# Long convolutions of a Hyena branch: signals kept channel-major, blocks folded about their middle, two matmuls per residue forward and 128-column inverses

## The chip, the cores and the metric

One Trainium2 core runs the whole kernel; the other seven are idle. The metric is the device time of one execution in microseconds (us). Engines: PE is the TensorE matmul array, DVE is VectorE, ACT is ScalarE, POOL is GpSimd, and SP issues nearly all DMAs, in order, from one queue.

## The reference, cut to what matters

One encoder layer runs on two groups of rows that share weights: a prompt of 512 positions and a sample of 1024 positions, 1024 features each. In each group a projection gives, among others, 1536 channels for the Hyena branch. Per channel and order, a signal is convolved with a long filter as long as the sequence in both directions, by a zero-padded FFT:

```python
def _fftconv(u, hf, skip):
    L = u.shape[1]
    uf = jnp.fft.rfft(u.astype(jnp.float32), n=2 * L, axis=1)
    y = jnp.fft.irfft(uf * hf[None], n=2 * L, axis=1)[:, :L]
    return y + u * skip

u = _dwconv(hy_in, hy_short_w, hy_short_b)          # 3 taps
v, x1, x2 = jnp.split(u, HYENA_ORDER + 1, axis=-1)  # 512 channels each
zb = x1 * _fftconv(v, filt[:, 0], hy_skip[0])
zb = x2 * _fftconv(zb, filt[:, 1], hy_skip[1])
y_b = jnp.einsum('blc,cd->bld', zb, hy_out_w)
```

Around it stand a 31-tap convolution branch, the gated sum of both branches, an output projection with a layer norm, and a squared-ReLU MLP with a layer norm. All of it is float32.

## The kernel before, in words

**The transform.** A signal of length L is cut into L/128 blocks of 128 positions (`nt`: 4 blocks for the prompt, 8 for the sample). The transform of length 2L is done in two steps. Butterflies over the blocks on DVE (`even8`, `odd8`, called by `fwd_bfly`) leave one complex block for each of 4 (prompt) or 8 (sample) residues of the frequency. Then each residue's block is multiplied on PE with 128x128 tables of cosines and sines (`fwd_mm`: four float32 matmuls per residue, two of them accumulating into the real part and two into the imaginary part). `conv_core` takes two residues at a time, loads the filter's spectrum `ks` from DRAM into a tile `sg`, and multiplies on DVE (two products and two sums per pair). `inv_mm` returns to blocks, `inv_bfly` undoes the butterflies and ends with the multiplication by x1 or x2.

**Layouts.** Before the change the signals are turned to positions on partitions: `to_tokens` transposes the output of the 3-tap convolution `conv3` (channels on partitions, tile `cv`) with PE and evicts it with ACT. The forward matmuls then have a table as the stationary operand and 128 channels as columns. The first convolution's inverse has again a table as the stationary operand (four matmuls of 128 columns per residue). The second one's inverse has the spectrum as the stationary operand and two tables side by side as columns (two matmuls of 256 columns), which gives channels on partitions. The tables are symmetric about a shift of the block (`fft_sym`), so that one table serves both directions.

**Work and order.** One group has four channel chunks of 128, so there are 4 x 2 convolutions for the prompt and as many for the sample. These convolutions, the filters' spectra (`filters`), the 31-tap convolution (`conv31`) and its norm are side work: Python generators in two lanes. Main work is the projections and the prompt's MLP, `mlp(gp)`. A `Meter` counts an estimated time for each DVE and PE instruction as it is written (DVE: 0.065 us plus a cycle per column, divided by `SHARE` = 0.88; PE by columns). After each main step, `pump` writes steps of side work as long as DVE's estimate is behind PE's:

```python
        while v.us < t.us:
            live = [i for i in range(2) if self.side[i]]
            if not live:
                break
```

So the estimates decide how far the side work is spread over the main work. Main work goes on through both input projections, the prompt's branches and output projection, and into `mlp(gp)`, which stops as soon as no side work is left; if side work is left when `mlp(gp)` has ended, it is written in a loop with no main work beside it:

```python
                while self.side[0] or self.side[1]:
                    self.step(min((i for i in range(2) if self.side[i]), key=lambda i: self.spent[i]))
```

Then the pools of the side work close and the sample's second half follows: `branches(gs)` first, which loads what the side work has left in DRAM (`d_ca` of the 31-tap branch, `d_zb` of the Hyena branch), splits each tile into a rounded part and a rest (ACT, then DVE, tiles `pg`), and starts its matmuls with them; then the output projection and the MLP by seven products. When `mlp(gp)` has steps left there, these loads and splits are written beside them. The framework gives each engine its own instruction list and waits by semaphores; engines run their lists in order. Pools are rings: `fx` has 3 PSUM banks, `sg` 6 buffers, `fp` 11, `so` 5.

Of the kernel before, what the change touches and what calls it, by code (L numbers as in the profile page):

```python
# [60 lines left out]
def fft_tables():  # L61


    n = np.arange(128)[:, None].astype(np.float64)
    k = np.arange(128)[None, :].astype(np.float64)
    h = k[:, :64]
    c0, s0 = np.cos(2 * np.pi * n * h / 128), np.sin(2 * np.pi * n * h / 128)
    s0[:, 0] = (-1.0) ** np.arange(128)
    c8, s8 = np.cos(2 * np.pi * n * (h + 0.5) / 128), np.sin(2 * np.pi * n * (h + 0.5) / 128)
    first = [np.hstack([c0, c8]), np.hstack([c0, -c8]), np.hstack([s0, s8]), np.hstack([s0, -s8])]  # L70
    w = np.ones((64, 1))
    w[0] = 0.5
    back = [np.vstack([w * c0.T, c8.T]), np.vstack([w * c0.T, -c8.T]), np.vstack([w * s0.T, s8.T]), np.vstack([w * s0.T, -s8.T])]
    plain, sym = list(first), first + back
    for k1 in TILES_S[1:]:
        d = k1 / 16.0
        for dst, e in ((plain, 0.0), (sym, d)):
            a = 2 * np.pi * np.fmod((n + e) * (k + d), 128.0) / 128
            c, s = np.cos(a), np.sin(a)
            dst += [-s, c, s] if k1 == 6 else [s, c, -s]  # L80
    return tuple(np.ascontiguousarray(np.stack(t, axis=1).astype(np.float32)) for t in (plain, sym))
# [80 lines left out]
class Enc:  # L162
# [135 lines left out]
    def fwd_mm(self, ti, ev, q, ps):  # L298
# [12 lines left out]
        else:  # L311
            o = self.fft0 + 3 * (ti - 1)
# [18 lines left out]

    def conv_core(self, g, o, c, ev, q):

        nc, v = self.nc, self.V
        ys = []
        kny = self.sm([1, CW], tag="kny")
        nc.sync.dma_start(kny, g.kny[o, c])
        for pr in range(len(g.tiles) // 2):
# [3 lines left out]
            for j in range(2):  # L342
                self.fwd_mm(2 * pr + j, ev, q, ps[:, j])
# [8 lines left out]
            ys.append(t1)  # L352
        return ys

    def inv_mm(self, g, ys, chan_major):

        nc, t, f = self.nc, self.T, self.fft
        outs = []
        for pr, y in enumerate(ys):
# [3 lines left out]
            for j in range(2):  # L363
                ti = 2 * pr + j
                yr, yi = y[:, j, 0], y[:, j, 1]
                if ti == 0:
                    m = 4
                    mr, mi = (m, m + 1), (m + 2, m + 3)
                else:
                    m = self.fft0 + 3 * (ti - 1)  # L370
                    mr, mi = (m + 1, m + 2), (m, m + 1)
                if chan_major:
                    p = ps[:, j].rearrange("p a b -> p (a b)")
# [1456 lines left out]
```

## Time and profile before

| what | value |
|---|---|
| median of 3 runs (lowest to highest) | 2349.55 us (2346.08 to 2349.87) |
| the profiled execution, its own time | 2351.76 us |
| its span, first to last instruction | 2350.0 us |
| PE busy | 2267.9 us (97%) |
| DVE busy | 1890.1 us (80%) |
| ACT busy | 920.5 us (39%) |
| mean granted TensorE clock | 0.993 |

The span is 1.8 us shorter than the profiled execution's own time; the median of the runs is 2.2 us below that own time. A float32 matmul stands in the profile as two records (768 in the program are 1536 in the trace), a transpose or a matmul of rounded (`fp32r`) tiles as one. Matmul records overlap: "mean ns of one" holds the way through the array too, so the cost of one in a row of many is read from how long the row of many takes.

### The profile page before, as it was taken

To read this page: it belongs to the slowest core of one execution; us is meant where nothing else is said; L and a number is where in the kernel's file an instruction comes from. 1 tells how busy PE (TensorE), PEld (TensorE's weight loads), DVE (VectorE), ACT (ScalarE), POOL (GpSimd) and SP (SyncE) were. 2 spreads that over 40 slices of the span, in tenths; PEclk is the share of its full clock that TensorE was granted. 3 is DMA by queue.
4 is the path that set the end of the run, shared out by engine and by line. 5 is a ranking of instruction groups with operands and counts; after the bars stand their busy time and mean duration, and the time that the engine had idled before them with its cause. 6 is when DMAs were issued, how large, how long until landed. Compare 5 with 4: busy or idle time off the path is not lost.

```text
span 2350.0 us, 33224 instructions
## 1 busy us (share of the span) xinstructions
PE 2267.9 (97%) x11684; PEld 1882.4 (80%) x11684; DVE 1890.1 (80%) x3662; ACT 920.5 (39%) x1521; POOL 54.3 (2%) x149
## 2 busy tenths in 40 slices
PE   6999999999999999989999999999999999999998
PEld 3878777778878888978888888789887777788886
DVE  5989797786989998895898875965987777577888
ACT  3464522422232223356543344222574444444430
POOL 2210100000000000000000000000000000000000
PEclk9999999999999999999999999999999999999999
DMA  6555434564356646634443344653675666876631
GB/s 246 179 169 175 138 113 163 195 224 159 133 188 203 200 174 215 218 116 144 144 135 99 94 157 154 210 156 109 210 247 188 215 205 214 283 241 215 205 124 71
DMA packets 201068, 412.80 MB, mean 176 GB/s; under 512 B 23321, under 2 KB 33739, under 8 KB 200389
## 3 DMA queue, kind: packets, MB, share of 16 engines
q1 hardware_dynamic: 200069, 409.67, 53.0%
q8 instruction: 92, 1.51, 0.3%
q0 software_dynamic: 832, 1.02, 0.2%
q14 instruction: 75, 0.61, 0.1%
HBM read 316.16 MB, written 94.43 MB: 175 GB/s over the span
## 4 chain that ended last, share of the span: by engine, by line
PE 79%; DVE 9%; DMA 8%; ACT 2%; issue 2%; SPq 1%; DVEq 0%; ACTq 0%
PE mm L145 57%; PE fx L145 19%; PE tr L145 3%; DVE sg L145 2%; DVE pg L145 2%; DVE wt L145 1%; DMA fp<-in_dec_s_dram 1%; DMA sg<-d_xs 1%; DMA fp<-in_w_ada_dram 1%; DVE st L145 1%; DVE fp L145 1%; DMA sg<-in_ffn_w_dram 1%; DMA sg<-ks 1%; DMA raw<-in_w_out_dram 1%; DVE xt L145 1%
## 5 line engine op out<-in xcount | busy, mean ns | idle before, releaser
L145 PE MATMUL mm<-pg,wt 128*128 128x512 f32 (+1 forms) x4776 | 1139.7, 391 | 5.0 <-DVE xt L145 3.6
L145 PEld LDWEIGHTS mm<-pg,wt 128*128 128x128 f32 x4776 | 878.7, 189 | 194.4 <-issue 11.9
L145 PE MATMUL mm<-wt,pg 128*128 128x512 f32 (+1 forms) x2556 | 480.8, 344 | 9.5 <-DVE wt L145 5.0
L145 PEld LDWEIGHTS mm<-wt,pg 128*128 128x128 f32 x2556 | 404.8, 190 | 68.6 <-DVE wt L145 6.8
L202 ACT ACTIVATE wt<-raw 128x512 fp32r<-128x512 f32 x430 | 268.7, 630 | 476.1 <-PE mm L145 375.7
L145 DVE TENSOR_TENSOR wt<-raw,wt 128x512 fp32r<-128x512 f32 x430 | 290.2, 684 | 80.0 <-ACT wt L202 78.1
L145 DVE SCALAR_TENSOR_TENSOR cv<-cv,pp 128x512 f32<-128x512 f32 (+1 forms) x288 | 288.7, 1009 | 7.3 <-ACT cv L853 2.3
L145 PEld LDWEIGHTS fx<-fp,fft 128*128 128x128 f32 x1536 | 177.5, 192 | 20.2 <-issue 15.1
L145 PE MATMUL fx<-fp,fft 128*128 128x128 f32 x1536 | 184.1, 277 | 1.7 <-DVE sm L145 1.1
L145 DVE TENSOR_TENSOR fp<-fp 128x256 f32<-128x256 f32 (+2 forms) x328 | 145.0, 481 | 15.6 <-ACT fp L380 10.2
L145 DVE TENSOR_TENSOR sg<-fx,sg 128x512 f32<-128x512 f32 (+1 forms) x162 | 98.6, 629 | 43.9 <-PE fx L145 27.7
L145 DVE TENSOR_TENSOR pg<-so,pg 128x512 fp32r<-128x512 f32 (+1 forms) x162 | 99.6, 623 | 38.3 <-ACT pg L202 26.9
L145 PE MATMUL fx<-pg,pg 128*128 128x512 f32 x492 | 120.7, 394 | 7.2 <-ACT pg L202 4.3
L145 PEld LDWEIGHTS fx<-pg,pg 128*128 128x128 f32 x492 | 93.5, 190 | 27.5 <-ACT pg L202 4.7
L202 ACT ACTIVATE pg<-so 128x512 fp32r<-128x512 f32 (+1 forms) x127 | 72.1, 575 | 73.9 <-DVE so L145 52.0
L145 PE MATMUL fx<-wt,pg 128*128 128x512 f32 x387 | 95.5, 389 | 0.0
L1260 ACT ACTIVATE so<-so,pp 128x512 f32<-128x512 f32 x62 | 44.4, 719 | 128.8 <-DVE so L145 128.7
L145 DVE TENSOR_TENSOR sg<-sg 128x256 f32<-128x256 f32 (+2 forms) x187 | 82.3, 460 | 6.4 <-ACT sg L890 5.0
L145 PEld LDWEIGHTS fx<-wt,pg 128*128 128x128 f32 x387 | 72.7, 188 | 15.1
L145 PE MATMUL mm<-pg,pg 128*128 128x512 f32 x300 | 73.9, 396 | 5.5 <-DVE xt L145 5.5
L380 ACT ACTIVATE fp<-fx 128x512 f32<-128x512 f32 x48 | 28.7, 598 | 120.6 <-PE fx L145 110.4
L145 DVE TENSOR_TENSOR pg<-pg,pg 128x1024 fp32r<-128x1024 f32 (+1 forms) x45 | 55.0, 1221 | 24.4 <-ACT pg L202 19.6
(175 smaller groups left out, 2221.4 us busy)
## 6 DMA issues: line engine op xcount, KB each, us to landing
raw<-in_mlp_w_dram SPq DMA_DIRECT2D x232, 256.0 KB
raw<-in_w_in_dram SPq DMA_DIRECT2D x144, 256.0 KB
xr<-in_mlp_w_dram SPq DMA_DIRECT2D x104, 256.0 KB
fp<-in_w_ada_dram SPq DMA_DIRECT2D x48, 512.0 KB
pg<-d_p SPq DMA_DIRECT2D x44, 512.0 KB
raw<-in_w_out_dram SPq DMA_DIRECT2D x64, 256.0 KB
d_p<-so SPq DMA_DIRECT2D x64, 256.0 KB
d_g<-so SPq DMA_DIRECT2D x48, 256.0 KB
```

Source lines behind the costliest of these rows:

```text
L145: return f(*args, **kw)
L202: self.nc.scalar.activation(hi, src, AF.Copy)
L380: nc.scalar.activation(outs[-1][:, 4 * (pr % 2):4 * (pr % 2) + 4].rearrange("p (j w) c -> p j w c", j=2), ps, AF.Copy)
L1260: nc.scalar.activation(out, src, AF.Relu, bias=self.pp[:, C_B1 + f:C_B1 + f + 1], scale=1.0)
```

## The change

Signals stay with channels on partitions. `fold` adds and subtracts, within each block, the first 64 positions and the last 64 read backwards (two DVE instructions over all blocks), so each block holds its even and its odd part about its middle. The butterflies run on that. Then PE transposes the butterflies' output, 16 blocks for the sample, 8 for the prompt, and ACT evicts each PSUM bank in two halves of 64 partitions, the lower half with its two blocks swapped. With the real part's cosine and the imaginary part's sine stacked in one table, a residue needs two forward matmuls of 128 columns (four for residue 0). The inverse always has the spectrum as the stationary operand and one table of 128 columns, two matmuls per residue, written into PSUM as two runs of 64 columns that lie apart for all residues but some. `inv_bfly` is as before; `unfold` adds and subtracts the halves again (two DVE instructions) and multiplies by x1 or x2, which stays in the tile of `conv3`. `to_tokens` is gone. The generator `hyena` hands back at more places and without numbers (they weren't used). The second table becomes `fft_sig`: 34 blocks of 128 columns where `fft_sym` had 29.

```diff
+    c, s, no = np.hstack([c0, c8]), np.hstack([s0, s8]), np.zeros((64, 128))
+    fwd = [np.vstack([c, no]), np.vstack([np.hstack([c0, -c8]), no]), np.vstack([no, np.hstack([s0, -s8])]), np.vstack([no, s])]
+    inv = [np.block([[w * c0.T, w * c0.T], [c8.T, -c8.T]]), np.block([[w * s0.T, w * s0.T], [s8.T, -s8.T]])]
...
+        a = 2 * np.pi * m * (k + d) / 128
+        c, s = np.cos(a), sign * np.sin(a)
+        fwd += [np.vstack([c, -s]), np.vstack([c, s])]
+        inv += [np.hstack([c.T, -s.T]), np.hstack([s.T, c.T])]
...
+    def fold(self, g, src):
...
+        a, b = src[:, :, 0:64], src[:, :, 127:63:-1]
+        v.tensor_tensor(x[:, 0:g.nt, 0:64], a, b, op=ALU.add)
+        v.tensor_tensor(x[:, 0:g.nt, 64:128], a, b, op=ALU.subtract)
+        return x
...
+        for pr in range(npr):
+            if pr % 2 == 0:
+                turned.append(self.fp())
+            src = q if pr >= 2 else ev
+            ps = self.fx_ps([128, 2, 2, 128])
+            for j in range(2):
+                for n, slot in enumerate(self.SLOTS[TILES_S[2 * pr + j]]):
+                    self.T.transpose(ps[:, j, n], src[:, slot], self.ident)
+            dst = turned[-1][:, 4 * (pr % 2):4 * (pr % 2) + 4].rearrange("p (j n) c -> p j n c", j=2)
+            nc.scalar.activation(dst[0:64], ps[0:64], AF.Copy)
+            nc.scalar.activation(dst[64:128], ps[64:128, :, ::-1], AF.Copy)
+        yield
...
-                self.fwd_mm(2 * pr + j, ev, q, ps[:, j])
+                x = turned[pr // 2][:, 4 * (pr % 2) + 2 * j:4 * (pr % 2) + 2 * j + 2]
+                for n in range(2):
+                    if pr == j == 0:
+                        self.T.matmul(ps[:, j, n], f[:, 2 * n], x[:, 0], start=True, stop=False)
+                        self.T.matmul(ps[:, j, n], f[:, 2 * n + 1], x[:, 1], start=False, stop=True)
+                    else:
+                        self.T.matmul(ps[:, j, n], f[:, 2 + 2 * (2 * pr + j) + n], x[:, n], start=True, stop=True)
...
-                if chan_major:
-                    p = ps[:, j].rearrange("p a b -> p (a b)")
-                    t.matmul(p, yr, f[:, mr[0]:mr[0] + 2].rearrange("p a b -> p (a b)"), start=True, stop=False)
-                    t.matmul(p, yi, f[:, mi[0]:mi[0] + 2].rearrange("p a b -> p (a b)"), start=False, stop=True)
-                else:
-                    for w in range(2):
-                        t.matmul(ps[:, j, w], f[:, mr[w]], yr, start=True, stop=False)
-                        t.matmul(ps[:, j, w], f[:, mi[w]], yi, start=False, stop=True)
+                p = ps[:, j].rearrange("p w (h n) -> p (w h) n", h=2)
+                for n, to in enumerate((slice(0, 3, 2), slice(1, 4, 2)) if ti == 0 else (slice(0, 4, 3), slice(1, 3))):
+                    self.T.matmul(p[:, to], y[:, j, n], f[:, 18 + 2 * ti + n], start=True, stop=True)
...
+    def unfold(self, g, e, mul):
...
+        a, b = e[:, 0:g.nt, 0:64], e[:, 0:g.nt, 64:128]
+        v.tensor_tensor(y[:, 0:g.nt, 0:64], a, b, op=ALU.add)
+        v.tensor_tensor(y[:, 0:g.nt, 127:63:-1], a, b, op=ALU.subtract)
+        v.tensor_tensor(y[:, 0:g.nt], y[:, 0:g.nt], mul, op=ALU.mult)
+        return y
...
-        x = self.to_tokens(g, self.conv3(g, c))
...
-        x1 = self.to_tokens(g, self.conv3(g, 4 + c))
...
+        z = blocks(self.conv3(g, c))
+        yield
+        for o in range(2):
+            x = self.fold(g, z[:, 0:g.nt])
+            yield
+            ev, q = self.fwd_bfly(g, x)
+            yield
+            ys = yield from self.conv_core(g, o, c, ev, q)
+            outs = self.inv_mm(g, ys)
+            m = blocks(self.conv3(g, 4 * (o + 1) + c))
+            yield
+            z = self.inv_bfly(g, outs, m)
+            yield
```

The instruction counts of the two programs differ so: PE has 768 -> 608 float32 matmuls fx<-fp,fft (the filters' 384 among them are untouched), 192 matmuls fx<-sg,fft of 128 columns and 96 fx<-fft,sg of 256 columns -> 192 fx<-fft,sg of 128 columns (112 of them as two runs of 64), 96 transposes fx<-ident,cv -> 192 fx<-ident,fp. DVE has 64 more instructions, 32 of 256 and 32 of 512 elements. ACT has 24 evictions fewer of 512 elements on 128 partitions and 96 more on 64 partitions.

What the estimates make of it, on PE's list. Here is the end of the side work in the program before: the last sample convolution (fx<-fp,fft is its forward, fx<-fft,sg its inverse) in the middle of `mlp(gp)`, whose matmuls are mm<-pg,wt (up) and mm<-wt,pg (down).

```order
L145 MATMUL mm<-pg,wt 128x512 x24
L145 MATMUL fx<-fp,fft 128x128 x32
L145 MATMUL fx<-fft,sg 128x256 x4
L145 MATMUL mm<-pg,wt 128x512 x4
L145 MATMUL fx<-fft,sg 128x256 x8
L145 MATMUL mm<-pg,wt 128x512 x4
L145 MATMUL fx<-fft,sg 128x256 x4
L145 MATMUL mm<-pg,wt 128x512 x64
L145 MATMUL mm<-wt,pg 128x512 x96
L145 MATMUL mm<-pg,wt 128x512 x96
L145 MATMUL mm<-wt,pg 128x512 x96
```

And here is the place in the changed program where the side work ends: the last matmuls of `mlp(gp)` (mm<-wt,pg and mm<-pg), then transposes and forward matmuls of a convolution; the sixteen inverse matmuls are cut. This piece from the first fx<-ident,fp on stands three times in a row on PE, and what follows the third is the first matmul of `branches(gs)`.

```order
L158 MATMUL mm<-wt,pg 128x512 x9
L158 MATMUL mm<-pg 128x512 x3
L158 MATMUL fx<-ident,fp 128x128 x16
L158 MATMUL fx<-fp,fft 128x128 x18
L158 MATMUL fx<-fft,sg 128x2x64 x3
L158 MATMUL fx<-fft,sg 128x128
L158 MATMUL fx<-fft,sg 128x2x64
```

Before, 520 matmuls of `mlp(gp)` come behind the last convolution (the last four rows above and 168 more). Now none do: three of the eight sample convolutions (the second of channel chunk 2 and both of chunk 3) come behind the last of them.

On DVE, the end of the last sample convolution before: the butterflies (fp<-fp), the multiplication by x2 (fp<-fp,cv), among splits for the MLP's weights (wt) and activations (pg) and additions of `mlp(gp)`'s results (pg<-pg,mm), with the first splits for `branches(gs)` (numbered pg) between them.

```order
L145 SCALAR_TENSOR_TENSOR fp<-fp 128x4x128
L145 TENSOR_TENSOR wt<-raw,wt 128x512
L145 SCALAR_TENSOR_TENSOR fp<-fp 128x2x128
L145 TENSOR_TENSOR wt<-raw,wt 128x512 x2
L145 TENSOR_TENSOR fp<-fp,cv 128x1024
L145 TENSOR_TENSOR pg<-so,pg 128x512
...
L145 TENSOR_TENSOR pg<-pg,mm 128x512
L145 TENSOR_TENSOR pg_13200<-so,pg_13200 128x512
L145 TENSOR_TENSOR pg<-pg,mm 128x512
L145 TENSOR_TENSOR pg_13205<-so,pg_13205 128x512
```

And the same place now: the end of the last one but one (its unfold, 128x8x64, and the multiplication), the fold of the last (128x8x64 again), and further down that one's end, directly followed by the sixteen splits for `branches(gs)`, which no other work stands between.

```order
L158 SCALAR_TENSOR_TENSOR fp<-fp 128x4x128
L158 SCALAR_TENSOR_TENSOR fp<-fp 128x2x128
L158 TENSOR_TENSOR fp<-fp 128x8x64 x2
L158 TENSOR_TENSOR fp<-fp,cv 128x1024
L158 TENSOR_TENSOR fp<-fp 128x8x64 x2
L158 TENSOR_TENSOR fp<-fp 128x512 x2
...
L158 TENSOR_TENSOR fp<-fp,cv 128x1024
L158 TENSOR_TENSOR pg_14083<-so,pg_14083 128x512
L158 TENSOR_TENSOR pg_14088<-so,pg_14088 128x512
L158 TENSOR_TENSOR pg_14093<-so,pg_14093 128x512
```

On DVE's list, between the last addition of `mlp(gp)` and that last multiplication, stand besides the three convolutions: 3 instructions of `conv3` and 4 of the prompt's last layer norm (1024 elements each), 6 splits of weights (512), 2 BN_STATS, 1 BN_AGGR and about 25 one-column instructions.

## Rows read from the trace of the kernel before

**Rows 1.** The page, part 1 (busy us, share of the span, instructions of each engine) and part 2 (the span in 40 equal slices, busy share in tenths).

```profile
PE 2267.9 (97%) x11684; PEld 1882.4 (80%) x11684; DVE 1890.1 (80%) x3662; ACT 920.5 (39%) x1521; POOL 54.3 (2%) x149
...
PE   6999999999999999989999999999999999999998
...
DVE  5989797786989998895898875965987777577888
```

**Rows 2.** Busy time of each engine in three stretches of the span (start:end and length in us, then busy us and instructions of each engine, granted clock, DMA share, GB/s): the side work's stretch, the rest of `mlp(gp)` behind it, and the sample's second half.

```profile
430.00:1381.00 951.00, 924.41 (x5359) 789.64 (x5358) 816.04 (x1703) 335.49 (x569) 6.95 (x72) 0.99 0.49 161
1381.00:1502.60 121.60, 117.97 (x519) 96.99 (x518) 86.51 (x148) 52.58 (x90) 0.00 (x0) 1.00 0.57 184
1502.60:2350.00 847.40, 817.92 (x3941) 682.69 (x3939) 637.10 (x1124) 349.58 (x562) 0.00 (x0) 0.99 0.58 192
```

**Rows 3.** Groups of instructions by line, engine, operation and shape (count | busy us, mean ns of one | idle before, and what ended it): PE's groups of the convolutions, ACT's evictions behind them.

```profile
L145 PE MATMUL fx<-fp,fft 128*128 128x128 f32 x1536 | 184.1, 277 | 1.7 <-DVE sm L145 1.1 <-DVE fp L145 0.2
...
L145 PE MATMUL fx<-sg,fft 128*128 128x128 f32 x384 | 47.7, 276 | 2.5 <-DVE sg L145 2.5
...
L145 PE MATMUL fx<-fft,sg 128*128 128x256 f32 x192 | 46.8, 387 | 1.9 <-DVE sg L145 1.4 <-DVE sm L145 0.3
...
L145 PE MATMUL fx<-ident,cv 128*128 128x128 f32 x208 | 31.1, 275 | 0.1
...
L380 ACT ACTIVATE fp<-fx 128x512 f32<-128x512 f32 x48 | 28.7, 598 | 120.6 <-PE fx L145 110.4 <-issue 10.3
```

**Rows 4.** PE's instructions in order of time in the last two sample convolutions (start us, us of the row of xcount instructions).

```profile
1304.12 1.04 PE L145 MATMUL fx<-ident,cv 128*128 128x128 f32 x8
1304.91 11.14 PE L145 MATMUL mm<-pg,wt 128*128 128x512 f32 x48
...
1326.07 3.75 PE L145 MATMUL fx<-sg,fft 128*128 128x128 f32 x32
...
1363.85 7.30 PE L145 MATMUL fx<-fp,fft 128*128 128x128 f32 x64
...
1374.34 3.65 PE L145 MATMUL fx<-fft,sg 128*128 128x256 f32 x16
```

**Rows 5.** DVE's instructions in order of time in the last sample convolution, from its products to its last multiplication (start us, us, in brackets idle time before it and what ended it).

```profile
1370.17 1.29 DVE L145 TENSOR_TENSOR sg<-fx,sg 128x512 f32<-128x512 f32 x2 [1.29 <-DMA sg<-ks]
1371.49 0.76 DVE L145 TENSOR_TENSOR sg<-sg 128x256 f32<-128x256 f32 x2
...
1375.17 1.29 DVE L145 TENSOR_TENSOR sg<-fx,sg 128x512 f32<-128x512 f32 x2 [0.93 <-DMA sg<-ks]
1376.92 0.43 DVE L145 TENSOR_TENSOR sg<-fp 128x256 f32<-128x256 f32 x1 [0.46 <-ACT fp L380]
...
1378.94 0.48 DVE L145 TENSOR_TENSOR fp<-sg 128x128 f32<-128x128 f32 x2
...
1381.30 2.77 DVE L145 TENSOR_TENSOR fp<-fp 128x512 f32<-128x512 f32 x8 [0.53 <-ACT fp L380]
...
1388.30 1.22 DVE L145 TENSOR_TENSOR fp<-fp,cv 128x1024 f32<-128x1024 f32 x1
1389.44 0.68 DVE L145 TENSOR_TENSOR pg<-so,pg 128x512 fp32r<-128x512 f32 x1
```

**Rows 6.** Groups of DVE by shape, as in rows 3; the COPY reads its 1023 elements backwards.

```profile
L145 DVE TENSOR_TENSOR fp<-fp 128x512 f32<-128x512 f32 x100 | 63.9, 682 | 3.3 <-ACT fp L380 1.9 <-ACT fp L817 1.4
...
L145 DVE COPY fp<-fp 128x1023 f32<-128x1023 f32 x1 | 0.7, 694 | 0.0
```

**Rows 7.** The chain of work that ended last, in order of time, around the end of the side work (start us, us, what).

```profile
1366.38 3.70 DMA sg<-ks
...
1380.63 93.41 PE mm L145 x412
```

**Rows 8.** What PE waited for before instructions of `fx` (in total us, times, longest).

```profile
PE fx L145 <- DVE sg L145: 6.7, 9, 1.4
...
PE fx L145 <- DVE fp L145: 3.2, 4, 1.5
```

**Rows 9.** Two stretches of 5 us; in the first PE had only transposes for the prompt's first layer norm to do, with waits between them (columns as in rows 2: the first busy time is PE's, the number behind POOL's is the granted clock).

```profile
1045.00:1050.00 5.00, 2.62 (x16) 1.82 (x14) 5.00 (x21) 3.42 (x5) 0.00 (x0) 0.96 0.00 0
1050.00:1055.00 5.00, 4.98 (x28) 4.49 (x29) 4.12 (x15) 3.76 (x8) 0.00 (x0) 0.70 0.00 0
```

**Rows 10.** PE and DVE in order of time at the end of `mlp(gp)` and the start of `branches(gs)`; sm<-sm are one-column instructions of the prompt's last layer norm.

```profile
1496.64 0.21 DVE L145 TENSOR_SCALAR sm<-sm 128x1 f32<-128x1 f32 x1
1496.77 0.68 DVE L145 BATCH_NORM_STATS2 st<-pg 128x6 f32<-128x512 f32 x1
...
1500.12 1.28 DVE L145 SCALAR_TENSOR_TENSOR pg<-pg,sm 128x1024 f32<-128x1024 f32 x1
...
1501.31 0.15 DVE L145 TENSOR_SCALAR sm<-sm 128x1 int32<-128x1 int32 x1
...
1502.62 27.59 PE L145 MATMUL mm<-pg,wt 128*128 128x512 f32 x121
```

**Rows 11.** SP's queue in order of time, from the last result of the side work to the last load of it for `branches(gs)`.

```profile
1389.55 0.33 SPq L841 DMA_DIRECT2D d_zb<-fp  x1
...
1396.95 1.85 SPq L903 DMA_DIRECT2D so<-d_ca  x4
...
1410.36 3.03 SPq L903 DMA_DIRECT2D so<-d_zb  x4
```

More of the change, by code (lines that the diff above doesn't have):

```diff
@@ L330, in spectrum_to @@
             nc.sync.dma_start(g.ks[o, c, pr], kt)
+    def fold(self, g, src):
+        v = self.V
+        x = self.fp()
+        a, b = src[:, :, 0:64], src[:, :, 127:63:-1]
+        v.tensor_tensor(x[:, 0:g.nt, 0:64], a, b, op=ALU.add)
+        v.tensor_tensor(x[:, 0:g.nt, 64:128], a, b, op=ALU.subtract)
+        return x
     def conv_core(self, g, o, c, ev, q):
-        nc, v = self.nc, self.V
-        ys = []
+        nc, v, f = self.nc, self.V, self.fft
+        npr = len(g.tiles) // 2
         kny = self.sm([1, CW], tag="kny")
         nc.sync.dma_start(kny, g.kny[o, c])
-        for pr in range(len(g.tiles) // 2):
+        turned = []
+        for pr in range(npr):
[10 more added lines that the diff above has]
+        yield
+        ys = []
+        for pr in range(npr):
             kt = self.sg([128, 2, 2, CW])
@@ L352, in conv_core, with inv_mm @@
             ys.append(t1)
+        yield
         return ys
-    def inv_mm(self, g, ys, chan_major):
-        nc, t, f = self.nc, self.T, self.fft
+    def inv_mm(self, g, ys):
+        nc, f = self.nc, self.fft
         outs = []
@@ L806, in conv3 @@
         return t
[L808 to L818 removed]
     def hyena(self, g, c):
         nc = self.nc
[L823 to L842 removed]
+        blocks = lambda t: t.rearrange("p (a b) -> p a b", b=128)
+        z = blocks(self.conv3(g, c))
[10 more added lines that the diff above has]
+            z = self.inv_bfly(g, outs, m)
+            yield
+        nc.sync.dma_start(g.d_zb[c], z[:, 0:g.nt].rearrange("p a b -> p (a b)"))
     def conv31(self, g, c):
@@ L1769 @@
 _INS = ["x_prompt", "x_sample", "pp", "w_ada", "b_ada", "w_in", "w_y", "w_out", "mlp_w1", "mlp_w2", "ffn_w1", "ffn_w2", "ffn_w3",
-        "skip", "ln1_g", "ln1_b", "mlp_b2", "ln2_g", "ln2_b", "fft", "fft_sym", "z_p", "z_s", "dec_p", "dec_s"]
+        "skip", "ln1_g", "ln1_b", "mlp_b2", "ln2_g", "ln2_b", "fft", "fft_sig", "z_p", "z_s", "dec_p", "dec_s"]
 _OUTS = [((512, D), "float32"), ((1024, D), "float32")]
@@ L1808, in layout @@
         o[k] = i[k][0]
-    o["fft"], o["fft_sym"] = fft_tables()
+    o["fft"], o["fft_sig"] = fft_tables()
     for n, L in (("p", 512), ("s", 1024)):
```

76 lines of the change are left out of this document (20 added, 56 removed).

## Prediction

> **What bounds the kernel now.** First the busy shares: PE 97%, DVE 80%, and PE's slices stay at 9 or 8 nearly throughout [rows 1], so at first sight every microsecond taken from PE is a microsecond of time. Then the stretches: where the convolutions lie, from 430 to 1381 us, PE is busy for 924 of 951 us, but DVE for 816 (86%); it is the second limit there, 135 us behind [rows 2]. Then the chain: behind the last convolution it is an unbroken row of main matmuls, 412 in 93.4 us, 0.227 us each [rows 7]. So the side work ends early enough to leave PE something to do, and DVE's slowness costs nothing. That cover has to be watched, since the order of both programs is known.
>
> **What the change takes from PE.** Costs of one are read from rows of many: a record of a 128-column float32 matmul takes 7.30/64 = 0.114 us forward and 3.75/32 = 0.117 us inverse, one of 256 columns 3.65/16 = 0.228, a transpose (1304.91 - 1304.12)/8 = 0.099, say 0.11 [rows 4]. The groups' means are a little higher (184.1/1536 = 0.120, 31.1/208 = 0.150), since the ends of short rows count in them [rows 3]. Forward: 160 matmuls, 320 records, 36.5 us less. Inverse: 384 x 0.117 + 192 x 0.228 = 88.7 us before, 384 x 0.117 = 44.9 now, 43.8 less. Transposes: 96 more, 10.6 us. Together 69.7 us less on PE (73 by the groups' means, 66 if the short rows are worse than I read them). A matmul written as two runs of 64 columns is not in the trace; it lies between the contiguous one of 0.117 and the one with twice the columns, 0.228. I take 0.117: the runs are long, and the columns are the same.
>
> On this very term the Trainium skill speaks against the change: its page "PSUM — Partial Sum Buffer", Specifications (TRN2), says that an access pattern which isn't contiguous slows matmuls significantly. It gives no size and no run here shows one; it is a rival below.
>
> **What it adds to DVE.** A row of DVE instructions advances by 0.60 us per 512 elements (1.29 for two less 0.69), 0.34 per 256, 0.20 per 128, 1.14 per 1024 [rows 5], although each is listed with 0.68 [rows 6]. The 64 additions cost 32 x 0.34 + 32 x 0.60 = 30 us. Reading backwards isn't dearer: the reversed copy took 694 ns for 1023 elements, about the 682 of a sum of 512 [rows 6]. If it were, a step of 1.2 us would be the upper bound, 0.6 us more on each.
>
> **What else moves, at no cost.** ACT gets 96 evictions of 64 partitions for 24 of 128; at 0.60 us each [rows 3] that is 43 us on an engine that works 335 of 951 us there [rows 2]. The larger table (34 blocks for 29) loads under main matmuls. PE's new waits, transposes for the butterflies, take the place of the forward matmuls' waits for the same results, 3.2 us in all [rows 8]; I add 2 us.
>
> **What the order does with it.** The meter sees PE's side work cheaper and DVE's dearer, so it spreads the side work over more main work, and main work runs out: three sample convolutions stand behind the last matmul of `mlp(gp)`, alone. Before, 520 main matmuls came behind the last one. So most of PE's gain is handed to a stretch in which PE waits for DVE. Its length decides.
>
> One convolution costs DVE, by the code, 17 instructions of 512 elements, 31 of 256, 20 of 128, the last one of 1024 and a one-row product: 17 x 0.60 + 31 x 0.335 + 20 x 0.20 + 1.14 + 0.20 = 26.0 us. Of the first of the three, fold and butterflies (7.7 us) are done beforehand: 18.3. The other DVE work listed there: 7 x 1.19 + 6 x 0.60 + 2 x 0.60 + 0.12 and 25 one-column instructions at 0.13 [rows 10] = 16.6. Together 18.3 + 52.0 + 16.6 = 87 us.
>
> DVE will not be busy all the time. In the last convolution before, it waited 1.29 and 0.93 us for the spectrum `ks`, whose load takes 3.7 us [rows 7] and can start only when a ring buffer is free, and 0.46 and 0.53 for evictions: 3.2 us [rows 5]. New is the wait from the last butterfly to the first product, now that nothing stands between: 8 transposes and six matmuls, 8 x 0.11 + 12 x 0.114 = 2.25 us, with the hops some 2.5. So 5.7 us at full clock. PE works only some 9.6 us per convolution (16 x 0.11 + 36 x 0.114 + 32 x 0.117). Where it had just 2.6 of 5 us to do, its granted clock was 0.70 in the next 5 us, that is, part of the time at 1.2 instead of 2.4 GHz [rows 9]; I expect the lower level in much of the tail. The 2.25 us above and two inverses of a pair on the way (0.94 each) would take twice as long, 4.1 us more: 9.8. I take 8 for each of the last two and 3 for the first, where the norm's instructions fill in: 19. The tail is then 106 us (99 to 112).
>
> Behind it `branches(gs)` starts with nothing prepared: sixteen tiles are to be split, the first five loaded beforehand, and the last channel's result has to go to DRAM and back, two trips of about 3.7 us [rows 7]. Before, issuing these loads took from 1397 to 1413 us, under main matmuls [rows 11]. PE can do its 48 first matmuls (10.9 us) as they come. I take 6 us lost, 3 to 10.
>
> **The sum.** End of `mlp(gp)` before: 1502.6 us [rows 10]. Less 69.7, less PE's share of the three convolutions, which comes later (3 x 9.6 = 28.8), plus 2: 1406. Plus 106 plus 6, plus the unchanged rest of 847.4 us [rows 2]: 2365.5 us of span against 2350.0. With the 1.8 us around the span 2367.3, and since the median lies 2.2 us below the profiled execution, 2365 us: 0.7% slower than 2349.55. In short, 70 us gained on PE, and 112 us of DVE's and DMAs' time uncovered, of which PE would have had to do 29 anyway.
>
> **Rivals.**
> - *Same tail, but short enough (not slower).* Break-even is where tail and restart together take 2350 - 847.4 - 1406 = 96.6 us instead of 112. With DVE's 87 that leaves 10 us of waits. For it: 87 us is firm, and `ks` may come faster on a quiet queue, so that 3.2 us per convolution vanish; PE may keep its clock. Against it: the 2.25 us chain and the split restart can't vanish. With waits of 6 and a restart of 3: 2349; with 70 read as 76 on PE: 2343. Chance 0.27, half of it within 0.2%, which is what a measurement of this kernel tells from no change.
> - *A longer tail.* All `ks` loads and the stores of the norm share SP's one list; a store that waits for the norm holds the next `ks` back, 3.7 us a time, and the clock is down throughout. Four such waits and 25 of clock and chain: 2385 to 2393. Chance 0.12.
> - *DVE pays the full time.* In the tail neighbours depend on each other; the sum behind two products starts after their end (1371.49 after 1371.46) [rows 5]. At the listed durations (0.68, 0.42, 0.28) the 87 us are 106, and the time 2384. Chance 0.06. The Trainium skill, "VectorE: DVE Perf Modes", section "The DRAIN you can't avoid", has the next operation wait until the pipe is empty; by that it would be 2384. Rows 5 show 0.60 between independent ones, so the trace agrees only in part.
> - *Split runs of columns are slow.* If the 112 matmuls take twice as long, 224 x 0.114 = 26 us of the gain go: 2391. Chance 0.04.
> - *The gain is simply PE's.* With no tail it would be 2280. The order speaks against it: nothing else is written beside the three convolutions. Chance 0.02.
>
> My forecast (2355 to 2380) has 0.49. Slower by over 0.2%: 0.49 + 0.12 + 0.06 + 0.04 = 0.71; within: 0.14; faster: 0.15. The range 2343 to 2391 leaves out the ends of the first and second rival and the last one.
>
> **What would show it.** A stretch of some 105 us, from about 1406 to 1512, with DVE busy over 80% and PE about a quarter to a third (more where its clock is at the lower level), and before it PE as busy as now. fx<-fp,fft at 1216 records, fx<-fft,sg at 384 with about 0.117 each in long rows. I am wrong on the mechanism if that stretch is not there; on its size, if the three convolutions take under 27 or over 40 us each; on the upstream part, if `mlp(gp)` ends more than 10 us away from 1406.

## The result and the profile after

The changed kernel takes 2383.2 us, median of 2374.97 to 2386.84, beside 2349.4 for the kernel before: ratio 1.0142 (95% interval 1.0114 to 1.0170), 34 us or 1.4% slower. Forecast were 2365 us, range 2343 to 2391: the direction was right, the size less than half of it.

The page of the profiled execution: the busy line of the engines, then PE, DVE and the granted clock in 40 slices of 59 us.

```profile
PE 2227.4 (94%) x11268; PEld 1832.0 (77%) x11268; DVE 1923.1 (81%) x3726; ACT 966.0 (41%) x1593; POOL 54.1 (2%) x149
...
PE   6999999999999999899989994599999999999998
...
DVE  5988797878989999847779899765988777677887
...
PEclk9999999999999999999999997799999999999999
```

Beside [rows 1]: PE is busy for 40.5 us less and DVE for 33.0 more, and there is a hole in PE's slices, 4 and 5, with the clock at 7. Cut at the last main matmul of `mlp(gp)` and at the first of `branches(gs)`, this execution (span 2373.2) and a second one of the same kernel (2382.4) look like this (columns as in [rows 2]: length, busy PE, PEld, DVE, ACT, POOL, granted clock):

```profile
0.00:1422.80 1422.80, 1362.06 (x7076) 1112.39 (x7077) 1196.37 (x2393) 583.19 (x978) 53.95 (x147) 0.99 0.51 168
1422.80:1523.60 100.80, 43.21 (x254) 37.21 (x252) 90.30 (x232) 24.55 (x41) 0.13 (x2) 0.70 0.28 92
1523.60:2373.20 849.60, 822.16 (x3940) 682.41 (x3940) 636.41 (x1103) 358.28 (x575) 0.00 (x0) 0.99 0.59 194
```

```profile
0.00:1431.60 1431.60, 1366.62 (x7074) 1115.93 (x7075) 1196.25 (x2393) 583.38 (x978) 54.11 (x147) 0.98 0.50 167
1431.60:1532.60 101.00, 44.72 (x255) 38.24 (x254) 90.61 (x233) 24.55 (x41) 0.13 (x2) 0.68 0.28 92
1532.60:2382.40 849.80, 822.41 (x3940) 683.12 (x3940) 636.02 (x1103) 357.99 (x575) 0.00 (x0) 0.99 0.58 194
```

The tail (the stretch behind the last main matmul of `mlp(gp)`, in which the last three convolutions stand alone) is there and is the same in both, 101 us with DVE busy for 90. The 9 us between the two executions lie ahead of it, where PE idles 4 us more and stands 14 us longer at 1.2 GHz. For comparison, the kernel before up to its own end of `mlp(gp)`:

```profile
0.00:1502.60 1502.60, 1449.96 (x7744) 1199.68 (x7745) 1253.02 (x2539) 570.92 (x960) 54.26 (x149) 0.99 0.51 166
```

PE in order of time in the tail: the transposes that open the second and the third convolution, and the first main matmuls behind it.

```profile
1442.91 2.08 PE L158 MATMUL fx<-fft,sg 128*128 128x128 f32 x8 [1.26 <-DVE sg L158]
1458.47 2.23 PE L158 MATMUL fx<-ident,fp 128*128 128x128 f32 x8 [13.48 <-DVE fp L158]
...
1492.47 2.23 PE L158 MATMUL fx<-ident,fp 128*128 128x128 f32 x8 [11.86 <-DVE fp L158]
...
1523.61 11.23 PE L158 MATMUL mm<-pg,wt 128*128 128x512 f32 x37 [12.62 <-ACT pg L215]
```

From one opening to the next it is 35.5 and 34.0 us. Of the 57.6 us that PE waits in the tail, 25.3 are the two stretches from a convolution's last inverse to the next one's first transpose: butterflies, unfold, product, fold and butterflies again, all on DVE. The 12.6 behind the third convolution hold its butterflies, unfold and product, and then the start of `branches(gs)`.

DVE's own waits in the tail: for the forward matmuls, once in each of the three convolutions, and for ACT's first split for `branches(gs)`, which in turn waited for the store of the last result.

```profile
1427.71 0.69 DVE L158 TENSOR_TENSOR sg<-fx,sg 128x512 f32<-128x512 f32 x1 [0.41 <-PE fx L158]
...
1466.36 1.29 DVE L158 TENSOR_TENSOR sg<-fx,sg 128x512 f32<-128x512 f32 x2 [0.67 <-PE fx L158]
...
1500.42 1.29 DVE L158 TENSOR_TENSOR sg<-fx,sg 128x512 f32<-128x512 f32 x2 [3.33 <-PE fx L158]
...
1518.94 1.23 DVE L158 TENSOR_TENSOR fp<-fp,cv 128x1024 f32<-128x1024 f32 x1
1523.59 2.50 DVE L158 TENSOR_TENSOR pg<-so,pg 128x512 fp32r<-128x512 f32 x4 [3.42 <-ACT pg L215]
```

```profile
1522.92 2.71 ACT L215 ACTIVATE pg<-so 128x512 fp32r<-128x512 f32 x5 [11.30 <-DMA d_zb<-fp]
```

New is also a long wait of the main matmuls well ahead of the tail. PE and then DVE from 1253 to 1267 us, in `mlp(gp)`, with two stretches of 5 us:

```profile
1253.98 4.60 PE L158 MATMUL mm<-wt,pg 128*128 128x512 f32 x19
1263.30 2.93 PE L158 MATMUL mm<-wt,pg 128*128 128x512 f32 x6 [4.72 <-DVE wt L158]
```

```profile
1255.58 2.77 DVE L158 TENSOR_TENSOR fp<-fp 128x512 f32<-128x512 f32 x8
...
1260.74 0.70 DVE L158 TENSOR_TENSOR wt<-raw,wt 128x512 fp32r<-128x512 f32 x1
1261.34 1.30 DVE L158 TENSOR_TENSOR fp<-fp 128x512 f32<-128x512 f32 x2
1262.55 0.70 DVE L158 TENSOR_TENSOR wt<-raw,wt 128x512 fp32r<-128x512 f32 x1
```

```profile
1260.00:1265.00 5.00, 1.70 (x4) 1.41 (x5) 5.00 (x9) 0.00 (x0) 0.13 (x2) 0.59 0.28 79
1265.00:1270.00 5.00, 5.00 (x17) 3.96 (x17) 5.00 (x11) 0.00 (x0) 0.00 (x0) 0.72 0.85 288
```

DVE is at 100%. The low halves of two weight pieces stand in its queue behind inverse butterflies, the second also behind the two additions of the unfold; PE runs dry for 4.7 us, and the trace's clock stands at 1.2 GHz for 6.8 us from 1260.9 on. Of these 4.5 lie behind the wait, where PE works at half speed, which costs another 2.2.

PE's waits of this kind (main matmuls that wait for a low half from DVE) up to the end of `mlp(gp)`, in total us, times and longest: in the kernel before, then in the first and in the second execution of the changed one.

```profile
PE mm L145 <- DVE wt L145: 2.3, 5, 0.8
...
PE mm L158 <- DVE wt L158: 10.3, 3, 4.7
...
PE mm L158 <- DVE wt L158: 9.7, 3, 4.7
```

They grew by 8.0 us, and PE's whole idle time there by 8.1 (60.7 against 52.6). In the second execution it is 7.4 of 12.3; there the loads for the filters' part (sg<-d_t) cost 6.5 us of waiting beside 0.9 before.

### The profile page after: what moved, and what is told of

Its sections match the earlier page's. It is cut to its first block, busy times and chain, and to the rows that moved or that the text cites. A ratio compares the mean times of both kernels' runs of the same rounds, so it can differ in the third digit from the quotient of the medians.

```text
span 2373.2 us, 32531 instructions
## 1 busy us (share of the span) xinstructions
PE 2227.4 (94%) x11268; PEld 1832.0 (77%) x11268; DVE 1923.1 (81%) x3726; ACT 966.0 (41%) x1593; POOL 54.1 (2%) x149
## 3 DMA queue, kind: packets, MB, share of 16 engines
q1 hardware_dynamic: 200069, 410.32, 52.6%
## 5 line engine op out<-in xcount | busy, mean ns | idle before, releaser
L158 PE MATMUL mm<-wt,pg 128*128 128x512 f32 (+1 forms) x2556 | 485.7, 346 | 16.4 <-DVE wt L158 12.9
L158 DVE SCALAR_TENSOR_TENSOR cv<-cv,pp 128x1024 f32<-128x1024 f32 (+1 forms) x288 | 290.3, 1015 | 13.6 <-ACT cv L842 7.7
L158 DVE TENSOR_TENSOR fp<-fp 128x256 f32<-128x256 f32 (+2 forms) x368 | 163.3, 486 | 7.1 <-ACT fp L414 6.6
L158 PEld LDWEIGHTS fx<-fp,fft 128*128 128x128 f32 x1216 | 146.2, 196 | 19.1 <-issue 10.9
L158 PE MATMUL fx<-fp,fft 128*128 128x128 f32 x1216 | 152.9, 281 | 5.7 <-DVE sm L158 2.9
L1282 ACT ACTIVATE so<-so,pp 128x512 f32<-128x512 f32 x62 | 44.4, 719 | 128.2 <-DVE so L158 128.1
L158 PEld LDWEIGHTS mm<-pg,pg 128*128 128x128 f32 x300 | 55.2, 188 | 21.7 <-DVE xt L158 10.5
```

Source lines behind the costliest of these rows:

```text
L158: return f(*args, **kw)
L1282: nc.scalar.activation(out, src, AF.Relu, bias=self.pp[:, C_B1 + f:C_B1 + f + 1], scale=1.0)
```

## The experiments

Theory A is the prediction's: PE's saving comes out in full ahead of the tail, and the tail is the loss. B says that VectorE bounds the whole stretch with side work, so that the tail's work costs the same wherever it lies. C, put after the first runs, says that the tail is a loss, and that its DVE work costs PE waits wherever DVE is already full. `SHARE` and `V.share` are the pump's credit for a DVE microsecond: the larger, the earlier side work is taken. Differences between versions are taken from their ratios to the kernel before, times 2349 us; each ratio is known to about 0.002, so such a difference is known to about 6 us.

**1. The tail undone by order.** From `mlp(gp)` on the pump takes side work faster; the order of PE ahead of that is untouched.

```diff
-                mlp = self.mlp(gp)
+                mlp = self.mlp(gp); self.V.share = 1.05
```

> The changed kernel, but from the start of mlp(gp) on the pump credits a VectorE microsecond with 1.05 in place of 0.88, so that it takes more side work per matmul there; the rows of PE up to that place are the same, and the side work ends 297 main matmuls before mlp(gp) does, with no sample convolution left alone behind it. Theory A (the tail is the loss): the 100.8 us of tail and the 8 of restart go, and about 24 us of PE work of the three convolutions comes back under mlp(gp): some 2295 to 2310 us, ratio to the kernel before 0.977 to 0.984. Rival B (VectorE is the bound, at 88 to 92% in the last 220 us of mlp(gp) already): the 90 us of VectorE work pushed in there turn into waits of PE of the same size, 2345 to 2380 us, ratio 0.998 to 1.013.

> The same edit with 0.96: one sample convolution of 50 PE records is left alone instead of three. Theory A: two thirds of the convolutions' price of some 26 us each goes, the restart stays: 2325 to 2340 us, ratio 0.990 to 0.996. Rival B: 2360 to 2385 us, mlp(gp) ends later by what the tail is shorter.

> The changed kernel with the pump's credit at 1.00 from the start of mlp(gp) on (0.96 left one convolution alone and gave 2349 us, 1.05 left none and gave 2342 with VectorE at 98% from 1200 to 1350 us): the side work ends 68 main matmuls before mlp(gp). If both prices, the restart behind a lone convolution and the waits where VectorE is full, are what is left, this lies at the best place between: 2332 to 2342 us, ratio 0.993 to 0.998. If the waits follow VectorE's work alone, wherever it is put: 2342 to 2349 us.

With 0.96 (one convolution alone) 2349.45, ratio 1.0000 (0.9986 to 1.0015); with 1.00 (none) 2347.56, 0.9995 (0.9983 to 1.0008); with 1.05 2341.94, 0.9976 (0.9958 to 0.9994), the only version here with the whole computation that lies below both kernels clear of noise, by 0.2%. So undoing the tail returns 33 to 39 us, and with 1.05 A had promised 73 to 88; B's range for it is missed by 3 us. A hundred microseconds in `mlp(gp)` with 1.05, and PE's longest wait in them:

```profile
1200.00:1300.00 100.00, 79.19 (x418) 66.13 (x416) 97.93 (x229) 38.74 (x63) 0.53 (x8) 0.86 0.28 95
```

```profile
1219.03 3.35 PE L158 MATMUL mm<-wt,pg 128*128 128x512 f32 x7 [10.78 <-DVE pg L158]
```

DVE is 98% busy and PE 79%, at a clock of 0.86: the tail's work went into the places where DVE had no room.

**2. The credit changed in the whole program** (`SHARE = 0.88` to 0.92 and 1.00).

> The changed kernel with the pump's credit for VectorE at 0.92 in place of 0.88 in the whole program, so that the side work is taken a little faster from the start and ends 247 main matmuls before mlp(gp) does; no sample convolution stands alone. Theory C (after the runs with the credit raised from mlp(gp) on alone: the tail is lost time, but its 90 us of VectorE work cost PE waits wherever VectorE is at 97% already, as it was at 1200 to 1350 us there): spread over the whole program the same work falls where VectorE has room (60 to 85% at 430 to 1200 us), so better than 2342 us: 2315 to 2335. Theory A in its old form (PE's work alone is left): 2295 to 2310. Rival B (VectorE bounds the whole side window, wherever its work lies): 2342 us or more.

> The same with 1.00: the side work ends 925 main matmuls before mlp(gp) does. Theory C: too much of it now lies ahead of mlp(gp), where the pump asks for more VectorE time than there is, so PE waits there and VectorE idles behind: 2320 to 2350 us, not better than with 0.92. Theory A in its old form: the same as 0.92, within 5 us, since no tail is left in either.

2346.95 us, ratio 0.9998 (0.9989 to 1.0008), and 2392.4, 1.0196 (1.0177 to 1.0215). Against Theory C as I had put it, and with 0.92 in the range of B: there is no roomy place to spread to. With 1.00 PE waits 38 us for low halves of weights (`mm` for DVE `wt`), half of it from 1000 to 1150 us, and from 1400 to 1500 DVE is busy for 44 of 100.

**3. A tail in the kernel before** (the same edit of `V.share`, with 0.72, in the old kernel).

> The kernel before, without the change, but with the credit lowered from 0.88 to 0.72 from the start of mlp(gp) on: two of its own sample convolutions (112 PE records) are left alone behind the last main matmul; nothing else is changed. Theory A: each costs 28 to 32 us alone less some 9 us of PE work that mlp(gp) no longer holds, and the restart some 6 to 8: slower by 45 to 55 us, 2395 to 2405 us, ratio 1.019 to 1.023. Rival B (order does not matter because VectorE is the bound): within 10 us of the kernel before.

2379.4 us, ratio 1.0131 (1.0101 to 1.0162): slower by 31 us, less than the 45 to 55 expected and far from nothing. Its two stretches:

```profile
0.00:1465.40 1465.40, 1416.84 (x7511) 1170.60 (x7512) 1203.05 (x2412) 556.01 (x933) 54.17 (x149) 0.99 0.50 164
1465.40:1521.30 55.90, 34.54 (x235) 31.78 (x233) 52.46 (x143) 7.67 (x14) 0.00 (x0) 0.87 0.34 106
```

Two convolutions alone take 55.9 us and the restart 10.8 (858.2 left, against 847.4 in [rows 2]), but `mlp(gp)` ends 37 us sooner without their PE work and waits. A tail by itself is a loss, also without the change: 15 us for each convolution.

**4. DVE's additions taken away, and doubled.** In one kernel `fold` and `unfold` issue no half additions, in the other each twice:

```diff
-        v.tensor_tensor(x[:, 0:g.nt, 0:64], a, b, op=ALU.add)
-        v.tensor_tensor(x[:, 0:g.nt, 64:128], a, b, op=ALU.subtract)
+        v.us += 2 * vector_cost((a,)) / v.share      # x = src; unfold likewise
```

> The changed kernel without the four half additions of each convolution (64 VectorE instructions, about 30 us by the prediction's sum); the pump still counts them, so that the order stays. The folding is left out of the computation, and nothing takes its place. Theory C (the upstream loss is VectorE's: with the additions doubled the last matmul of mlp(gp) ended at 1436 in place of 1422): mlp(gp) ends 10 to 14 us earlier than with the additions and the tail is 7 to 10 us shorter: 2360 to 2368 us, ratio 1.005 to 1.008. Rival E (the upstream loss is TensorE's, whose saving is smaller than the 69.7 us of the sum): mlp(gp) ends within 5 us of where it did, and only the tail is shorter: 2371 to 2378 us.

> The changed kernel with each of the four half additions of a convolution issued twice, the second time over the same result and not counted by the pump: 64 VectorE instructions more, about 30 us by the prediction's sum. Theory A (only the tail and a few waits ahead pay for VectorE): the tail grows by three times 2.4, upstream by 2 to 4: slower than the changed kernel by 8 to 12 us, ratio to the kernel before 1.017 to 1.020. Rival B (VectorE is the bound): slower by 25 to 35 us, ratio 1.025 to 1.030. Rival C (these additions cost nothing): no difference, 1.014.

Without them 2359.0 us, ratio 1.0055 (1.0037 to 1.0072): 20 us less for 29.9 us of DVE (page: 1893.2), C's case and not E's. Doubled 2393.9, 1.0197 (1.0171 to 1.0222): 13 us more for 26.9, at the upper end of A's range and far from B's. (The kernel without additions also takes one buffer of `fp` less for each convolution; the doubled one changes nothing but DVE's list.) The stretches without them, and PE's waits for low halves ahead of the tail:

```profile
0.00:1414.30 1414.30, 1355.71 (x7074) 1107.57 (x7075) 1174.79 (x2342) 582.82 (x978) 54.19 (x149) 0.99 0.51 170
1414.30:1501.50 87.20, 45.04 (x255) 38.89 (x253) 80.57 (x217) 24.43 (x41) 0.00 (x0) 0.71 0.28 91
```

```profile
PE mm L158 <- DVE wt L158: 5.8, 3, 2.8
```

The tail is 14 us shorter, and `mlp(gp)` ends 8 to 17 us earlier than in the two executions with the additions. The time at 1.2 GHz ahead of that point is back at 17.1 us, as in the kernel before, against 30.7 and 44.4 with them. About half of the growth in the waits for low halves is gone.

**5. TensorE's saving given back** (each forward matmul but the first residue's issued twice).

> The changed kernel with each of the forward matmuls behind the transposes (but those of the first residue) issued twice, the second time over the same result and not counted by the pump: some 320 records at 0.117 us, 37 us of TensorE, about what the prediction says that the forward part saves. If TensorE bounds the part ahead of the tail, as the sum has it: mlp(gp) ends 25 to 30 us later and the tail grows by 5 to 10: 2413 to 2423 us. If VectorE bounds that part by now and TensorE has room: mlp(gp) ends 5 to 15 us later, 2393 to 2405 us.

2396.3 us, ratio 1.0210 (1.0195 to 1.0225): 16 us more for 320 records, 36.5 us of PE at the 0.114 of [rows 4] (29.3 by the busy lines, 2256.7 against 2227.4), so 0.44 to 0.55 for each. PE is no longer the sole limit there: part of what it is given to do fills waits.

**6. Both in the order without a tail** (credit 1.05 as in 1).

> The changed kernel with the pump's credit at 1.05 from mlp(gp) on (no convolution left alone, 2342 us) and without the four half additions of each convolution (64 VectorE instructions, some 33 us; the folding is left out of the computation and the pump still counts it). GpSimd could not show what relief of VectorE is worth, since VectorE's own instructions grew by what was taken off. If VectorE's work is what holds the end in this order too: 2312 to 2322 us, 0.6 to 0.9 us for each us. If TensorE's work holds it: 2333 to 2342.

> The mirror of that: the same order without a tail (2342 us), all additions in, and the forward matmuls behind the transposes issued twice, some 37 us of TensorE not counted by the pump. If VectorE holds the end in this order: 2342 to 2357 us, less than 0.4 us for each us. If TensorE holds it: 2365 to 2380 us, 0.6 us or more for each.

Without the additions 2323.4 us, ratio 0.9890 (0.9868 to 0.9913): 20 us less for 29.4 us of DVE, 0.69 for each. With the forward matmuls doubled 2358.6, 1.0044 (1.0029 to 1.0059): 16 us more, 0.44 to 0.48 for each (36.5 and 33.5 us). Both engines hold the end in this order too. Whether DVE holds it more firmly is not shown: with 6 us of noise in each difference the two shares overlap.

**7. ScalarE.** One eviction of 128 partitions for two of 64:

```diff
-            nc.scalar.activation(dst[0:64], ps[0:64], AF.Copy)
-            nc.scalar.activation(dst[64:128], ps[64:128, :, ::-1], AF.Copy)
+            nc.scalar.activation(dst, ps, AF.Copy)
```

> The changed kernel with one ScalarE eviction of 128 partitions for each pair of tiles after the transposes, in place of two of 64 partitions; the reversal of the lower half is left out of the computation. ScalarE loses 48 instructions of 0.59 us, 28 us. Rival D (ScalarE's extra evictions made the upstream loss): mlp(gp) ends 5 to 15 us earlier than at 1422.8 and the tail is some 2 us per convolution shorter: 2360 to 2372 us. Theory C (VectorE's load made it): mlp(gp) ends where it did within 4 us, the tail is 2 to 6 us shorter: 2375 to 2382 us.

2376.4 us, ratio 1.0130 (1.0114 to 1.0146): 3 us less for 31 us of ACT, within the noise. `mlp(gp)` ended at 1428.5, between the two executions with both evictions, so ACT's added work is not what delays it.

**8. GpSimd for VectorE.** First the half additions (`v.tensor_tensor` to `self.nc.gpsimd.tensor_tensor`), then, in both kernels, every third weight piece's low half:

```diff
+        if self.np_ % 3 < 1:
+            self.nc.scalar.activation(w[:, 0], raw, AF.Copy)
+            self.nc.gpsimd.tensor_tensor(w[:, 1], raw, w[:, 0].bitcast(F32), op=ALU.subtract)
```

> The changed kernel with the four half additions of each convolution (64 instructions) on GpSimd in place of VectorE, counted by the pump as before. VectorE loses some 33 us of work, 3.6 us of it in the tail's chain where GpSimd's own time stands instead; the trace has no such GpSimd addition (its memset of 1024 columns takes 0.96 us), so 0.5 to 2 us for each. Theory C (VectorE's load ahead of mlp(gp)'s end is what the upstream waits come from): mlp(gp) ends 5 to 15 us earlier than at 1422.8, the tail is 0 to 17 us longer: 2370 to 2390 us. Rival D (the upstream loss is ScalarE's, whose evictions rose by 51 us): mlp(gp) ends at 1420 to 1425 as before.

> The changed kernel with the low halves of every third streamed weight piece (143 of 430 subtractions of 0.688 us, 98 us of VectorE in the whole span, some 60 of them ahead of mlp(gp)'s end) on GpSimd; the pump no longer counts these, so it takes side work sooner and it ends 271 main matmuls before mlp(gp) does, with nothing left alone. Theory C (VectorE's load in the side window is what the saved TensorE time is lost to): no tail and fewer waits than the 2342 us of the kernel with credit 1.05: 2300 to 2325 us, ratio 0.980 to 0.990. Rival F (GpSimd's additions, 1.3 to 2.0 us each where they were tried, slow VectorE or bring the weights late): 2340 to 2380 us.

> The kernel before, with the same third of the weight pieces on GpSimd and without the change: what the relief of VectorE is worth by itself. Theory C: there TensorE bounds (49 us idle up to the end of the side work) and VectorE's load matters less: 2335 to 2350 us, ratio 0.994 to 1.000, so that the change with the relief is faster than the relief alone by 20 us or more. Rival F: slower than before, 2355 to 2380.

> The changed kernel with every second weight piece's low half on GpSimd (215 of 430, 148 us of VectorE); the side work ends 463 main matmuls before mlp(gp) does. Theory C: the same or 5 to 10 us better than with every third, 2295 to 2320. Rival F: worse than with every third by 10 us or more.

The first three are slower than any of the theories had them; the last came out as F said. The half additions on GpSimd: 2419.7 us, 1.0311 (1.0290 to 1.0332); each takes 1.3 to 2.0 us at 512 elements (means of groups), and DVE waits 28 us for those of the unfold, with its queue behind it. The weight pieces: 2386.1, 1.0158 (1.0137 to 1.0179), and in the kernel before 2397.1, 1.0208 (1.0192 to 1.0224); with every second piece 2411.2, 1.0265. Groups and busy line of the changed kernel with every third piece moved:

```profile
L158 DVE TENSOR_TENSOR wt<-raw,wt 128x512 fp32r<-128x512 f32 x308 | 225.7, 739 | 76.7 <-ACT wt L215 75.3
L236 POOL TENSOR_TENSOR wt<-raw,wt 128x512 fp32r<-128x512 f32 x122 | 211.9, 1737 | 1093.7 <-ACT wt L235 983.9 <-issue 28.2 <-DVE so L158 18.9
...
PE 2241.8 (94%) x11268; PEld 1837.7 (77%) x11268; DVE 1923.7 (81%) x3604; ACT 965.9 (41%) x1595; POOL 265.7 (11%) x271
```

122 instructions fewer, 84 us by their mean of 688 ns, and DVE is as busy as ever, 1923.7 against 1923.1: its other instructions became longer, the 308 left in this group 739 for 688 ns and others with it. The Trainium skill, "SBUF — State Buffer", section "SBUF: two separate sides", says that VectorE with two inputs in SBUF and GpSimd lock one pair of ports against each other for a whole instruction; that agrees with these rows in kind. So these runs say nothing on what relief of DVE is worth; experiments 4 and 6 do. The time itself moved for the order as well, since the pump doesn't count the moved instructions.

**9. TensorE's clock in the tail.** Six matmuls that nobody reads behind each step of the lone convolutions.

> The changed kernel with six idle matmuls of 128 columns behind each step of the three convolutions that stand alone, some 120 in all, so that TensorE has work where it waits for VectorE; they read the tables and nobody reads them. If the clock, 0.70 in the tail and 0.85 or less around it, is a good part of the tail's price: the granted clock there comes out above 0.9, and the tail of 101 us with the restart is 8 to 14 us shorter, 2369 to 2376 us. If VectorE's chain alone sets the tail, its clock costs little: within 5 us of 2382.

2382.2 us, ratio 1.0149 (1.0131 to 1.0167): no gain. Some of the idle matmuls were taken ahead of the tail; those in it, 130 records, all came to lie in the first of the three convolutions, which makes that one the test (the first row here; the second is the same convolution in the changed kernel):

```profile
1425.70:1462.00 36.30, 27.09 (x217) 25.01 (x216) 35.15 (x88) 9.63 (x15) 0.13 (x2) 0.92 0.45 150
```

```profile
1422.80:1458.50 35.70, 14.79 (x87) 13.01 (x85) 34.88 (x87) 9.63 (x15) 0.13 (x2) 0.67 0.46 153
```

At a granted clock of 0.92 in place of 0.67 the convolution takes 36.3 us in place of 35.7. DVE is busy for 35 of them either way, so PE's clock is not on this path. It is also the convolution in which DVE had the least to wait for (0.4 us for the forward matmuls); in the third, where it waits 3.3, the clock stayed low, and what it costs there this run doesn't test.

**10. The changed kernel once more.**

> The changed kernel once more, unchanged, since its profiled execution was the shortest of four (2374.97 against a median of 2383): the median comes out at 2381 to 2386 us. If the spread between executions lies upstream, mlp(gp) ends in this profile at 1426 to 1434 us with a tail of 99 to 103; if it lies behind, the end is at 1422 again and the part after the restart is longer than 850 us.

2382.0 us, ratio 1.0142 (1.0125 to 1.0159); its profile is the second one in the section on the result. The spread lies upstream.

## Why the prediction was right in direction and short in size

**PE's saving: right.** fx<-fp,fft has 1216 records and fx<-fft,sg 384. Up to the end of `mlp(gp)` 79.8 us are saved (1502.6 to 1422.8); hidden behind that are 8.1 us of idle time more (60.7 against 52.6, length less busy) and 5.8 for the lower clock (of the 30.7 us at 1.2 GHz PE is busy in 25.1, of the 17.1 before in 13.5; half of the 11.6 between them is lost): 93.7 us of work less, 94.9 in the second execution, where 98.5 were forecast (69.7 and the three convolutions' 28.8). Writing two runs of 64 columns shows no cost:

```profile
1173.92 2.90 PE L158 MATMUL fx<-fft,sg 128*128 128x128 f32 x24
```

2.90/24 = 0.121 us with the end of the row in it, beside 0.117 for contiguous columns [rows 4]. The trace doesn't tell the two kinds apart, but more than half of these matmuls (112 of 192 in the program) are written as two runs; at twice the time for those the mean would be above 0.17. The slowing of non-contiguous patterns that the Trainium skill states ("PSUM — Partial Sum Buffer", Specifications (TRN2)) does not show here for an output of two runs.

**DVE's additions: right.** 64 instructions and 33.0 us more, 30 forecast; 29.9 go when they are left out.

**The step that failed: "I add 2 us".** PE's added waits ahead of the tail and the clock lost in them cost 13.9 us in the one execution (8.1 of idle time, 5.8 of clock) and 23.9 in the other (12.3 and 11.6). Behind it stands the sentence that "DVE's slowness costs nothing" as long as PE has main work left. With DVE at 86% over 951 us [rows 2] (85% in the changed kernel, 807 us) and in order, it is full for stretches; a longer block of butterflies then holds up the low halves that the main matmuls need, and the longest of these waits are followed by time at 1.2 GHz. I had asked only what the convolutions' own matmuls wait for [rows 8], and those waits behaved as forecast (`fx` for DVE `sg` and `fp` 9.9 us before, 8.1 after). I had not asked what the main work waits for behind them on DVE: 2.3 us before, 10.3 and 9.7 after. Experiment 4 shows what the additions have in it: without them the two items are 6.0 and 0.8, so 7 to 17 us are theirs. Where the other 6.8 come from, no run shows. By the sign that I had set (`mlp(gp)` within 10 us of 1406), the upstream part was wrong in both executions.

**The tail: right in place and cause, too long by 9 us.** DVE is busy 90 us of the 101 (87 forecast). Of the 10.5 that it waits, 3.4 lie behind the last product and belong to the restart; the three convolutions end with that product at 1520.2, after 97.4 us with 7.1 of waits, where I had 106 with 19. I had charged 8 us to each of the last two and 3 to the first, but in the second as well as the first other DVE work (layer norm, `conv3`) stood where DVE would have waited for the forward matmuls: it waited 0.4 and 0.7 us there, and 3.3 only in the third, against 2.5 forecast at the full clock. The waits for `ks` were 0.4 to 0.6 us, one in each convolution, where the last one of the kernel before had 1.29 and 0.93 [rows 5]. The 4.1 us for PE's lower clock in each convolution were too much: the clock does fall to 0.70, but experiment 9 shows no price in the first, and in the third there is room for about 1 us. The restart was right: 3.4 and 2.2 (849.6 against 847.4) are 5.6 where I had 6. Together 103 where I had 112.

**The sum** 1406 + 106 + 6 + 847.4 = 2365.5 became 1422.8 + 100.8 + 849.6 = 2373.2, and 1431.6 + 101.0 + 849.8 = 2382.4 in the second execution, which is the one near the median. Upstream +17 and +26, tail and restart -9 in both.

**The rivals.** The short tail needed 96.6 us or less for tail and restart, with `mlp(gp)` at its end by 1406; it was 103, and 1406 was not kept. The longer tail lies nearest in time (2385 to 2393 us), but not in cause: the tail was shorter than the sum's, and none of DVE's waits for `ks` in it came near 3.7 us. Full durations on DVE are out: 90 us busy, not 106. And what I never gave a rival to is the important one: that the gain isn't waiting to be had by a better order. "Simply PE's" with no tail was put at 2280; the kernel without a tail takes 2342, and 2323 if the additions cost nothing. Why about half to two thirds of each DVE microsecond and about half of each PE microsecond come out, and not other shares, stays open.

## What to carry to other kernels

When the first engine is at 97% and the second at 86% of the same stretch, taking 70 us from the first and giving 30 to the second is a trade between two limits. Price both by experiment: issue the added work twice, and the saved work again. Look in the second engine's queue for what the main stream needs from it, since a longer block there costs a wait and then some time at the lower clock; and where a planner meters the work, see what stands alone at the end, but don't take its whole length for the gain of moving it.

## What was not expected of the hardware

- GpSimd relieved VectorE of 122 subtractions, 84 us by their mean, and VectorE's busy time did not fall at all.
- A convolution that stands alone, with VectorE busy for 35 us of it, doesn't get faster when TensorE is kept at the higher clock: 36.3 us at 0.92, 35.7 at 0.67.
- Two executions of one kernel differ by 9 us in one stretch, through 4 us of waits and 14 us more at 1.2 GHz, in 11.5 of which TensorE works: there the waits count about double.
